# The operands of an MLP made five steps ahead instead of four, the fifth pair in fixed buffers

## The chip, the cores and the metric

The kernel runs on one core of one Trainium2 chip. TensorE (PE) multiplies matrices; VectorE (DVE) and ScalarE (ACT) work element by element; GpSimd (POOL) here mostly issues transfers that add into a tile; SyncE (SP) issues the other transfers. The metric is the device time of one execution in microseconds (us), lower is better.

## What is computed

A two-layer encoder over 512 positions of width 1024: stick-breaking attention in layer 0, a gated linear recurrence (RG-LRU) in layer 1, and behind each a MLP with squared ReLU and 4096 inner features. The change touches the MLPs alone, and their seams to what comes next:

```python
def squared_relu_mlp(h, w1, w2):
    u = jax.nn.relu(h @ w1)
    return (u * u) @ w2

def reference(x, ...):
    for layer in range(2):
        h = rms_norm(x, norm_mix[layer])
        y = stick_breaking_attention(h, ...) if layer == 0 else rglru_block(h, w_in, ...)
        x = x + y
        h = rms_norm(x, norm_mlp[layer])
        x = x + squared_relu_mlp(h, mlp_w1[layer], mlp_w2[layer])
    return rms_norm(x, norm_final)
```

## The kernel before

**Three matmuls for one.** PE multiplies a rounded 32-bit type. Each operand is held as a high half (the value rounded by a cast on ACT, `wh` for a weight, `sh` or `bh` for an activation) and a low half (what the rounding left, a subtraction on DVE: `wl`, `sl`, `bl`). A product is high times high, low times high, high times low.

**Seven products for eight.** The MLP's 4096 features are worked through in four quarters of 1024. In each quarter the up product and the down product are done on 2 by 2 blocks with seven products P1 to P7 in place of eight, for two halves p (or g) of the weights. A step is one product of one half: "P1 1" is P1 of half 1. A quarter has 14 up steps (places 0 to 13: P1 P5 P6 P3 P7 P2 P4 for p = 0, then for p = 1) and 14 down steps (places 14 to 27, in the order of `ORDERS`); the first quarter's up part is done in another way, so its steps begin at place 14. A step number i counts from the first quarter's first down step; `STEPS // 2`, 14, is the second quarter's first up step.

**Weight blocks.** `load` asks SP for blocks of 512 KB (`b11`, `b12`, `b22`, each with a buffer of its own) at fixed places. P2's block `b21` goes to a tile `raw` of the pool `wpool` instead, which has three such tiles. `added` makes the sums of blocks that some products need: the block itself is overwritten, by DVE (`b<-b,b`) or, for P7 and P4, by a transfer that POOL issues and that adds what it reads from memory. `operand` then makes a pair `wh`, `wl`; there are four pairs in turn. The stages behind the MLP take their weights through `slab`, with the same pairs and the same three raw tiles: `w_in` behind layer 0.

**Order.** In `run`, slot i is: `load(i)`, then `leave(i - 1)`, then PE's matmuls of step i. `leave` takes a finished step's result out of PSUM (ACT copies, DVE sums, `collect` into the output `c`), then calls `prepare(ahead)`, which makes the operand of a later step, here four steps on, with the block sums due, and then does what is left: relu, square, and the halves of the squared activations (`split`, `split_slot`, whose `sl` the down steps read). On ACT and DVE the instructions of the MLP run strictly in the order in which they are written (class `Ordered`); each engine starts nothing before the instruction ahead of it. SP and POOL have orders of their own, and a transfer into a buffer waits until its former content has been read.

**The end of layer 0.** The last steps' `leave` finds no more operands to make. The next stage begins with two slabs of `w_in`, whose `wl` (line 251) stand in DVE's order among the last `collect`s; behind them come the sums into `x` (line 1426) and the halves `xg` (lines 166 and 167) that the new stage's matmuls (lines 257 to 259) read.

Of the kernel before, what the change touches and what calls it, by code (L numbers as in the profile page):

```python
# [13 lines left out]
F32R = mybir.dt.float32r  # L14
# [53 lines left out]
def hybrid_encoder(  # L68
# [739 lines left out]
    class Mlp:  # L808
# [28 lines left out]
        def __init__(self, ctx, layer):  # L837
            self.layer, self.sq, self.first = layer, Squares(), None
            self.V, self.A = Ordered(V), Ordered(A)
            self.mp = ctx.enter_context(tc.tile_pool(name=f"mlp{layer}", bufs=2))  # L840
            self.c = [
                self.mp.tile([P, 2, S], F32, tag=f"c{i}", name=f"c{i}", bufs=1) for i in range(4)
            ]
            self.begun, self.a, self.aside = set(), {}, {}
            self.turns = count(4 * layer)
            self.blocks = ExitStack()
            self.bp = self.blocks.enter_context(tc.tile_pool(name=f"blocks{layer}", bufs=2))
            self.u, self.lows, self.s3, self.slots = {}, {}, {}, None

            t = self.bp.tile([P, C // 2 * S + ASIDE], F32R, tag="s41", name="s41", bufs=1)  # L850
            self.s41 = t[:, : C // 2 * S].rearrange("p (k s) -> p k s", s=S)
# [237 lines left out]
            )  # L1089

        def operand(self, raw):
            pool = wpools[next(slabs) % len(wpools)]
            wh = pool.tile([P, C, P], F32R, tag="wh", name="wh")
            wl = pool.tile([P, C, P], F32R, tag="wl", name="wl")
            wh, wl = (t.rearrange("p (j k) f -> p j (k f)", j=2) for t in (wh, wl))
            self.A.copy(wh, raw)
            self.V.tensor_tensor(wl, raw, f(wh), ALU.subtract)
            return wh, wl
# [73 lines left out]
        def run(self, first, between, end):  # L1172
# [47 lines left out]
            def prepare(i):  # L1220

                if i < len(steps) and steps[i][0] == "up" and steps[i][3] == "P7":
                    return
                if i - 1 in range(len(steps)) and i - 1 not in made and i > 2:
                    make(i - 1)
                if i < len(steps) and steps[i][0] == "down":
                    add(i, 0)
                    if waiting and place(i) in (20, 22, 23):
                        self.split_slot(*waiting.pop(0))
                make(i)  # L1230
                for n in range(i + 1, i + 6):
                    add(n, n - i)
# [4 lines left out]

            def load(i):
                q4, at = steps[i][1], place(i)
                for do in self.aside.get(i, ()):  # L1240
                    do()

# [2 lines left out]
                elif at == 0:  # L1245
                    self.turns = count(4)
                    self.u.clear()
                    del self.a[1]
                elif at == 4:
                    units["down", q4] = self.from_down(q4)  # L1250
                    self.load(units["down", q4], (0, "b11"), (0, "b12"), (1, "b11"))
                elif at == 11:
                    self.load(units["down", q4], (1, "b12"), (0, "b22"), (1, "b22"))
                elif at == 14 and q4 == NQ - 1:
                    end.ready()
                elif at == 22 and q4 < NQ - 1:
                    units["up", q4 + 1] = self.from_up(q4 + 1)
                    self.load(units["up", q4 + 1], (0, "b11"), (0, "b12"), (0, "b22"), (1, "b11"))
                elif at == 25 and q4 < NQ - 1:
                    self.load(units["up", q4 + 1], (1, "b12"), (1, "b22"))  # L1260

            def leave(i):

                ahead = i + 4
                if i < 0:
                    return
                kind, q4, p, name = steps[i]
# [627 lines left out]
```

## Time and profile before

| what | us |
| --- | --- |
| median of 3 runs (lowest, highest) | 1002.76 (1002.46, 1003.22) |
| the profiled execution | 1003.18 |
| its span, first to last instruction | 1001.3 |
| PE busy in it | 983.0 |
| DVE busy | 858.0 |
| ACT busy | 715.4 |

The granted clock of TensorE was 0.999 of full speed over the span. The page groups the helper classes' instructions under line 798, so the tiles' names tell them apart. The groups and transfers of the MLPs' weights:

```profile
L798 ACT CAST wh<-b 128x1024 fp32r<-128x1024 f32 x168 | 173.7, 1048 | 99.6 <-DVE b L798 50.1
L798 DVE TENSOR_TENSOR wl<-b,wh 128x1024 fp32r<-128x1024 f32 x168 | 203.6, 1220 | 38.9 <-ACT wh L798 38.5
L798 DVE TENSOR_TENSOR b<-b,b 128x1024 f32<-128x1024 f32 x48 | 58.7, 1223 | 1.3
L798 ACT CAST wh<-raw 128x1024 fp32r<-128x1024 f32 x46 | 47.9, 1043 | 4.1 <-PE ps_acc L1135 4.0
b<-in_w_dn SPq DMA_DIRECT2D x48, 512.0 KB, 5.1
b<-in_w_up POOLq DMA_DIRECT2D x24, 512.0 KB, 5.8
```

A row of a group has the engine, the operation, output and inputs with their shapes, how many; then busy us and the mean of one in ns; then how long the engine stood idle just before them and on whose account. A row of transfers ends with its size and the median us from issue to landing. A row of a timeline has the start in us, the length of the run of equal instructions, the instruction, how many, and in brackets the idle time before it and what ended it. A row of waits has the instruction that waited, what released it, the sum, how many times and the longest.

### The profile page before, as it was taken

Reading aid. Unit: us, or ns where it says so; the run is one execution under the profiler, and the core shown is the slowest. Engines: PE = TensorE matmul, PEld = TensorE weight load, DVE = VectorE, ACT = ScalarE, POOL = GpSimd, SP = SyncE. Lnnn points to the kernel's source line nnn. Section 1 sums busy time; section 2 is a strip of 40 time slices with the busy share of each in tenths; the row PEclk is TensorE's granted clock in tenths of the full one; section 3 lists DMA queues with packets and bytes.
Section 4 is the critical chain, followed back from the end, with each engine's and each line's share of the span. In section 5 each row is a group of like instructions: output and inputs, shape, how many; then the busy total and the mean of one; then the engine's idle time right before and its main releaser. Section 6 shows DMA issues by size and latency. Waiting matters only on the chain.

```text
span 1001.3 us, 15918 instructions
## 1 busy us (share of the span) xinstructions
PE 983.0 (98%) x5836; PEld 884.0 (88%) x5836; DVE 858.0 (86%) x1152; ACT 715.4 (71%) x1110; POOL 176.4 (18%) x243
## 2 busy tenths in 40 slices
PE   9999999999999999999999999999999999999996
PEld 7889999888878988988988888888889989989985
DVE  6888787848898799799799799986887898998898
ACT  6777676836887774774775699975887774874865
POOL 0454444420000011011011220100011111111111
PEclk9999999999999999999999999999999999999999
DMA  7855454537637767777693474446548877977953
GB/s 230 216 146 148 106 153 109 160 117 256 174 87 198 169 160 198 169 163 194 169 239 88 128 191 126 124 157 223 122 95 219 212 142 202 249 141 199 229 107 106
DMA packets 71902, 165.72 MB, mean 166 GB/s; under 512 B 23824, under 2 KB 25104, under 8 KB 71824
## 3 DMA queue, kind: packets, MB, share of 16 engines
q1 hardware_dynamic: 59424, 123.54, 39.4%
q0 software_dynamic: 11680, 40.38, 24.0%
q8 instruction: 46, 0.75, 0.3%
q10 hardware_dynamic: 720, 0.79, 0.2%
q14 instruction: 32, 0.26, 0.1%
HBM read 139.51 MB, written 6.29 MB: 146 GB/s over the span
## 4 chain that ended last, share of the span: by engine, by line
PE 39%; DVE 25%; ACT 22%; issue 8%; DMA 6%; SPq 0%; ACTq 0%; POOL 0%; DVEq 0%; POOLq 0%
PE ps_t L1135 8%; DVE wl L798 6%; ACT wh L798 6%; PE ps_acc L1135 4%; DVE u L798 4%; ACT u L798 3%; PE ps_acc L1036 3%; DVE b L798 3%; PE ps_acc L257 3%; PE ps_acc L259 3%; PE ps_acc L258 2%; PE ps_z L1135 2%; ACT bh L798 2%; DVE c L798 2%; ACT L798 2%
## 5 line engine op out<-in xcount | busy, mean ns | idle before, releaser
L798 ACT CAST wh<-b 128x1024 fp32r<-128x1024 f32 x168 | 173.7, 1048 | 99.6 <-DVE b L798 50.1
L798 DVE TENSOR_TENSOR wl<-b,wh 128x1024 fp32r<-128x1024 f32 x168 | 203.6, 1220 | 38.9 <-ACT wh L798 38.5
L1113 POOL DMA_DIRECT2D b<-in_w_dn x40 | 35.0, 876 | 339.6 <-DVE b L798 153.1
L1036 PE MATMUL ps_z<-xg,wh 128*128 128x256 f32 x384 | 78.2, 277 | 1.0 <-ACT u L798 1.0
L257 PE MATMUL ps_acc<-xg,wh 128*128 128x512 f32 x200 | 79.1, 395 | 0.0
L259 PE MATMUL ps_acc<-xg,wh 128*128 128x512 f32 x200 | 75.8, 379 | 0.0
L258 PE MATMUL ps_acc<-xg,wl 128*128 128x512 f32 x200 | 75.8, 379 | 0.0
L251 DVE TENSOR_TENSOR wl<-raw,wh 128x512 fp32r<-128x512 f32 (+2 forms) x70 | 62.0, 911 | 15.1 <-ACT wh L249 14.8
L798 ACT ACTIVATE u<-u 128x512 f32<-128x512 f32 x100 | 63.2, 632 | 13.3 <-DVE u L798 11.6
L623 DVE TENSOR_TENSOR_SCAN scan<-keep,later 128x128 f32<-128x128 f32 (+1 forms) x64 | 59.3, 929 | 12.9 <-ACT keep L613 6.5
L1036 PE MATMUL ps_z<-xg,wl 128*128 128x256 f32 x240 | 66.0, 275 | 0.0
L1036 PEld LDWEIGHTS ps_z<-xg,wh 128*128 128x128 f32 x384 | 63.5, 192 | 1.7 <-ACT u L798 1.6
L249 ACT CAST wh<-raw 128x512 fp32r<-128x512 f32 (+2 forms) x70 | 50.5, 757 | 19.1 <-PE ps_acc L259 6.8
L627 POOL TENSOR_TENSOR w<-w,scan 128x128 f32<-128x128 f32 (+1 forms) x64 | 51.6, 807 | 53.6 <-DVE scan L623 50.6
L1036 PE MATMUL ps_acc<-xg,wh 128*128 128x256 f32 x288 | 60.5, 275 | 0.0
L798 DVE TENSOR_TENSOR b<-b,b 128x1024 f32<-128x1024 f32 x48 | 58.7, 1223 | 1.3
L798 DVE TENSOR_TENSOR u<-u 128x512 f32<-128x512 f32 (+1 forms) x92 | 54.8, 595 | 2.3 <-ACT u L798 1.0
L1113 POOL DMA_DIRECT2D b<-in_w_up x24 | 20.9, 869 | 196.8 <-DMA b<-in_w_up 84.4
L1036 PE MATMUL ps_acc<-xg,wl 128*128 128x256 f32 x192 | 52.8, 275 | 0.0
L1036 PE MATMUL ps_acc<-low,wh 128*128 128x256 f32 x192 | 52.8, 275 | 0.0
L798 ACT CAST wh<-raw 128x1024 fp32r<-128x1024 f32 x46 | 47.9, 1043 | 4.1 <-PE ps_acc L1135 4.0
L1135 PE MATMUL ps_t<-wh,sl 128*128 128x512 f32 x126 | 48.5, 385 | 1.9 <-DVE sl L798 1.9
(372 smaller groups left out, 3257.9 us busy)
## 6 DMA issues: line engine op xcount, KB each, us to landing
b<-in_w_dn SPq DMA_DIRECT2D x48, 512.0 KB, 5.1
b<-in_w_dn POOLq DMA_DIRECT2D x40, 512.0 KB, 5.5
b<-in_w_up SPq DMA_DIRECT2D x36, 512.0 KB, 4.7
b<-in_w_up POOLq DMA_DIRECT2D x24, 512.0 KB, 5.8
raw<-in_w_m SPq DMA_DIRECT2D x16, 512.0 KB, 4.7
raw<-in_w_dn SPq DMA_DIRECT2D x16, 512.0 KB, 4.9
raw<-in_w_in SPq DMA_DIRECT2D x16, 512.0 KB, 4.2
raw<-in_w_qk SPq DMA_DIRECT2D x12, 512.0 KB, 3.7
```

Source lines behind the costliest of these rows:

```text
L249: A.copy(wh[:, k, :], raw[:, k, :])
L251: V.tensor_tensor(wl[:, k, :], raw[:, k, :], f(wh[:, k, :]), ALU.subtract)
L257: PE.matmul(ps, wh, ah, start=start, stop=False)
L258: PE.matmul(ps, wl, ah, start=False, stop=False)
L259: PE.matmul(ps, wh, al, start=False, stop=stop)
L623: V.tensor_tensor_scan(sc[:, S - n : S][:, ::-1], keep[:, :n][:, ::-1], later[:, S - n :][:, ::-1], 1.0, ALU.mult, ALU.max,)
L627: G.tensor_tensor(wt, wt, sc[:, S - n + 1 : S + 1], ALU.mult)
L798: ins = getattr(self.e, name)(*args, **kwargs)
L1036: PE.matmul(as_read(ps[:, i * HS : (i + 1) * HS]), m, turns_of(y), start=new and i == k == n == 0, stop=i == 1 and k == C // 2 - 1 and n == 2,
L1113: G.dma_start(out=unit[b].rearrange("p j n -> p (j n)"), in_=unit["src"](to), accum_op=ALU.add)
L1135: PE.matmul(ps, m, y[:, jj], start=first and n == 0, stop=last and n == 2, skip_group_check=not new,)
```

## The change

From the second quarter's first up step on, `leave` prepares five steps ahead. Every fifth operand from then on (the 15th, counted from nought, and so on) takes a fixed pair `spare` in place of the turn's; it lies in two of the three raw tiles and stays there to the end of the MLP. The places at which `split_slot` is called in `prepare` and the blocks are asked for are moved on or back by one, so that `split_slot` stays in the same slot and the blocks are asked for one slot sooner. `operand` takes the pairs from `wpool` directly, where it counted with `slab` before; the list of pools had one member.

```diff
-            self.turns = count(4 * layer)
+            self.turns, self.operands, self.spare = count(4 * layer), count(), None
...
         def operand(self, raw):
-            pool = wpools[next(slabs) % len(wpools)]
-            wh = pool.tile([P, C, P], F32R, tag="wh", name="wh")
-            wl = pool.tile([P, C, P], F32R, tag="wl", name="wl")
+            n = next(self.operands)
+            if n >= self.STEPS // 2 and n % 5 == 0:
+                if self.spare is None:
+                    self.spare = [
+                        wpool.tile([P, C, P], F32R, tag="raw", name="spare", bufs=3) for _ in range(2)
+                    ]
+                wh, wl = self.spare
+            else:
+                wh = wpool.tile([P, C, P], F32R, tag="wh", name="wh")
+                wl = wpool.tile([P, C, P], F32R, tag="wl", name="wl")
...
-                    if waiting and place(i) in (20, 22, 23):
+                    if waiting and place(i) in (21, 23, 24):
                         self.split_slot(*waiting.pop(0))
...
+                sooner = i >= self.STEPS // 2
...
-                elif at == 4:
+                elif at == 4 - sooner:
...
-                elif at == 11:
+                elif at == 11 - sooner:
...
-                elif at == 22 and q4 < NQ - 1:
+                elif at == 22 - sooner and q4 < NQ - 1:
...
-                elif at == 25 and q4 < NQ - 1:
+                elif at == 25 - sooner and q4 < NQ - 1:
...
-                ahead = i + 4
+                ahead = i + (5 if i >= self.STEPS // 2 else 4)
```

What this does to the engines' orders, at three places. First DVE at the end of the up part in layer 0's last quarter, before the change; `ps_o` is PE's sum for P3 in the first row and for P2 in the eighth, the last row's `sl` is the one made from P2's result:

```order
L798 TENSOR_TENSOR u_5617<-ps_o_5652,u_5617 128x512
L798 TENSOR_TENSOR wl_5753<-b11_5505,wh_5752 128x1024
L798 TENSOR_TENSOR b11_5505<-b11_5505,b12_5507 128x1024
L798 TENSOR_TENSOR u_5618<-u_5618,u_5619 128x512
L798 TENSOR_TENSOR sl_5786<-u_5617,sh_5785 128x2x256
L798 TENSOR_TENSOR wl_5790<-b11_5505,wh_5789 128x1024
L798 TENSOR_TENSOR sl_5786<-u_5618,sh_5785 128x2x256
L798 TENSOR_TENSOR u_5616<-u_5616,ps_o_5799 128x512
L798 TENSOR_TENSOR wl_5826<-b11_5509,wh_5825 128x1024
L798 TENSOR_TENSOR b11_5509<-b11_5509,b12_5745 128x1024
L798 TENSOR_TENSOR sl_5786<-u_5616,sh_5785 128x2x256
```

The same engine and place with the change:

```order
L798 TENSOR_TENSOR b11_5456<-b11_5456,b12_5458 128x1024
L798 TENSOR_TENSOR bl_79<-u_5367,bh_78 128x1024
L798 TENSOR_TENSOR u_5591<-ps_o_5636,u_5591 128x512
L798 TENSOR_TENSOR spare_3839<-b11_5456,spare_3838 128x1024
L798 TENSOR_TENSOR u_5592<-u_5592,u_5593 128x512
L798 TENSOR_TENSOR sl_5764<-u_5591,sh_5763 128x2x256
L798 TENSOR_TENSOR wl_5768<-b11_5460,wh_5767 128x1024
L798 TENSOR_TENSOR b11_5460<-b11_5460,b12_5692 128x1024
L798 TENSOR_TENSOR sl_5764<-u_5592,sh_5763 128x2x256
L798 TENSOR_TENSOR u_5590<-u_5590,ps_o_5776 128x512
L798 TENSOR_TENSOR wl_5805<-raw_5802,wh_5804 128x1024
L798 TENSOR_TENSOR sl_5764<-u_5590,sh_5763 128x2x256
```

Each weight half and each add has moved one slot forward: the first add stands ahead of P3's sum, the second ahead of P2's sum, where it stood behind it.

Second ACT in the second quarter of layer 0, the first in which five ahead holds. The copies of `ps_acc` are those of P1, P5 and P6, and the last that of P7; `b11_3745` is the block into which a transfer of POOL's adds. Before:

```order
L798 COPY u_3879<-ps_acc_3880 128x2x256
L798 COPY u_3879<-ps_acc_3906 128x2x256
L798 CAST wh_3932<-b12_3747 128x1024
L798 CAST wh_3938<-raw_3936 128x1024
L798 COPY u_3879<-ps_acc_3880 128x2x256
L798 CAST wh_3967<-b11_3745 128x1024
L798 CAST wh_4002<-b11_3751 128x1024
L798 ACTIVATE u_3879<-u_3879 128x2x256 x2
L798 COPY u_3879<-ps_acc_3880 128x2x256
```

The same with the change:

```order
L798 COPY u_3879<-ps_acc_3880 128x2x256
L798 CAST wh_3906<-b12_3747 128x1024
L798 CAST wh_3912<-raw_3910 128x1024
L798 COPY u_3879<-ps_acc_3916 128x2x256
L798 CAST spare_3838<-b11_3745 128x1024
L798 COPY u_3879<-ps_acc_3880 128x2x256
L798 CAST wh_3975<-b11_3751 128x1024
L798 CAST wh_4005<-b11_3751 128x1024
L798 ACTIVATE u_3879<-u_3879 128x2x256 x2
L798 COPY u_3879<-ps_acc_3880 128x2x256
```

The cast of `b11_3745` has moved ahead of P6's copy, and a cast of an added block (the second of `b11_3751`) ahead of P7's.

Third SP at the end of layer 0, before the change; `x` are rows of the residual that come back from memory, `raw<-in_w_in` the next stage's slabs:

```order
L243 DMA raw_6173<-in_w_in 128x1024
L1449 DMA x_5866<-away_3141 128x512
L1449 DMA x_5868<-away_3141 128x512
L1066 DMA b22_5749<-in_w_dn 128x1024
L1449 DMA x_5870<-away_3141 128x512
L243 DMA raw_6179<-in_w_in 128x1024
L243 DMA raw_6265<-in_w_in 128x1024
```

With the change:

```order
L1457 DMA x_5848<-away_3141 128x512
L1112 DMA raw_5992<-in_w_dn 128x1024
L243 DMA raw_6141<-in_w_in 128x1024
L243 DMA raw_6147<-in_w_in 128x1024
L243 DMA raw_6233<-in_w_in 128x1024
```

The first slab stood ahead of three other loads and now stands behind them and behind the last block `b21` of the MLP (`raw_5992`), with which it shares the one raw tile that is left. Where these slabs' `wl` stand on DVE with the change:

```order
L798 TENSOR_TENSOR spare_3839<-raw_5992,spare_3838 128x1024
L798 TENSOR_TENSOR wl_6009<-b11_5456,wh_6008 128x1024
L798 SCALAR_TENSOR_TENSOR c1_3132<-ps_acc_5883,rr_3492,c1_3132 128x512
L798 SCALAR_TENSOR_TENSOR c1_3132<-ps_acc_5884,rr_3492,c1_3132 128x512
L798 TENSOR_TENSOR wl_6027<-b11_5460,wh_6026 128x1024
L798 SCALAR_TENSOR_TENSOR c3_3134<-ps_t_5864,rr_3492,c3_3134 128x512
L251 TENSOR_TENSOR wl_6144<-raw_6141,wh_6143 128x1024
L798 SCALAR_TENSOR_TENSOR c3_3134<-ps_t_5865,rr_3492,c3_3134 128x512
L798 SCALAR_TENSOR_TENSOR c0_3131<-ps_z_5922,rr_3492,c0_3131 128x512
L798 SCALAR_TENSOR_TENSOR c0_3131<-ps_z_5923,rr_3492,c0_3131 128x512
L251 TENSOR_TENSOR wl_6150<-raw_6147,wh_6149 128x1024
L798 SCALAR_TENSOR_TENSOR c2_3133<-ps_t_5864,rr_3492,c2_3133 128x512
```

The next rows are the sums into `x` (line 1426 before, 1434 with the change), as they were; of the slabs' two `wl`, the first has moved ahead of one `collect`, the second stands where it stood.

## Prediction

> **What bounds the kernel now.** I read the page first (busy shares), then PE's waits, then the timelines of PE, DVE and ACT around them.
>
> ```profile
> PE 983.0 (98%) x5836; PEld 884.0 (88%) x5836; DVE 858.0 (86%) x1152; ACT 715.4 (71%) x1110; POOL 176.4 (18%) x243
> PE ps_t L1135 <- DVE sl L798: 1.9, 6, 0.3
> PE ps_z L1036 <- ACT u L798: 0.8, 2, 0.6
> ```
>
> TensorE (PE) is busy for 98% of the span; the change leaves its matmuls as they are, so only its waits can move. Those in the MLPs are short (the last row is of the window from 555 to 900 us alone). PE stands for `sl` (the low half of the squared activations) once in each of six quarters. The last quarter of layer 0 shows how:
>
> ```profile
> 513.99 0.38 PE L1135 MATMUL ps_t<-wl,sh 128*128 128x512 f32 x1
> 514.69 0.48 PE L1135 MATMUL ps_t<-wh,sl 128*128 128x512 f32 x1 [0.32 <-DVE sl L798]
> 515.01 0.38 PE L1135 MATMUL ps_t<-wh,sh 128*128 128x512 f32 x1
> 516.95 0.38 PE L1135 MATMUL ps_z<-wh,bh 128*128 128x512 f32 x1
> 517.42 0.48 PE L1135 MATMUL ps_z<-wl,bh 128*128 128x512 f32 x1
> 517.74 0.38 PE L1135 MATMUL ps_z<-wh,bl 128*128 128x512 f32 x1
> ```
>
> Undisturbed, these matmuls start every 0.216 us (nine of them from 515.01 to 516.95). In step "P1 1" (product P1, half 1) the one due at 514.21 came at 514.69, 0.48 late, and the next lost 0.10 more. In "P2 0" the second lost 0.25, the third 0.10. That is 0.94 us a quarter, of which only 0.35 is for a weight half `wl`, what the change makes earlier; 0.58 is for `sl`.
>
> **Where the late `sl` comes from.** DVE, then ACT, in the same quarter:
>
> ```profile
> 493.03 1.76 DVE L798 TENSOR_TENSOR bl<-u,bh 128x1536 fp32r<-128x1536 f32 x1 [1.48 <-ACT bh L798]
> 494.70 1.22 DVE L798 TENSOR_TENSOR wl<-b,wh 128x1024 fp32r<-128x1024 f32 x1
> 495.84 2.86 DVE L798 TENSOR_TENSOR u<-u 128x512 f32<-128x512 f32 x4
> ...
> 504.29 0.69 DVE L798 TENSOR_TENSOR u<-ps_o,u 128x512 f32<-128x512 f32 x1
> 504.89 1.22 DVE L798 TENSOR_TENSOR wl<-b,wh 128x1024 fp32r<-128x1024 f32 x1
> 506.14 1.22 DVE L798 TENSOR_TENSOR b<-b,b 128x1024 f32<-128x1024 f32 x1
> ...
> 510.35 0.69 DVE L798 TENSOR_TENSOR sl<-u,sh 128x512 fp32r<-128x512 f32 x1 [0.61 <-ACT sh L798]
> 510.96 0.68 DVE L798 TENSOR_TENSOR u<-u,ps_o 128x512 f32<-128x512 f32 x1
> ...
> 512.81 1.23 DVE L798 TENSOR_TENSOR b<-b,b 128x1024 f32<-128x1024 f32 x1
> 513.95 0.68 DVE L798 TENSOR_TENSOR sl<-u,sh 128x512 fp32r<-128x512 f32 x1
> ```
>
> ```profile
> 511.67 1.30 ACT L798 ACTIVATE u<-u 128x512 f32<-128x512 f32 x2 [0.41 <-DVE u L798]
> 513.00 0.62 ACT L798 CAST sh<-u 128x512 fp32r<-128x512 f32 x1
> ```
>
> From 493.03 to 514.63 DVE stands for 0.61 us only: here DVE's queue is the limit. The `u` of 510.96 (P2's sum) releases ACT's relu and square, these `sh`, and that the `sl` at 513.95, whose end at 514.63 PE waits for.
>
> **Part 1, five steps ahead, in a settled quarter: +0.8 us.** No instruction is added. What moves one step forward is each cast, its `wl` and the add behind it (`b<-b,b`). In DVE's order the `wl` of 494.70 goes before the `bl`, so the four sums follow at 494.65. Behind them now stand `wl` three times, `bl`, `wl`, the add of a step further, `bl` (today `wl` twice, `bl`, `wl`, `bl`). Behind such an operation the next starts 1.14 us later (512.81 to 513.95), the add 1.25 behind the `wl` that still reads its block (504.89 to 506.14). So `u<-ps_o,u` comes at 505.5 instead of 504.29. Its relu, square and `sh` (1.30 + 0.62) end at 508.2, `sl` follows; the next `wl` waits for its cast (1.05) until 509.2, then stands an add (1.25), a `sl`, and P2's `u` at 512.2, against 510.96. Relu, square and `sh` then end at 514.85 and `sl` at 515.55. It is only 0.9 late against 514.63 because today's `sl` waits behind the add of 512.81, which is now past. PE loses those 0.9 at "P1 1" and wins the 0.35 at "P2 0": +0.55. A second place adds 0.25: in the slot behind "P5 0" the add, its cast and the `wl` into the fixed pair now follow each other, with 1.1 us of DVE idle, and the `sl` that "P6 1" needs at about 526.05 ends near 526.3. So +0.8 a quarter; the ends are +0.4 (no second wait) and +1.2 (P4's step waits as well, for a copy that now stands behind a cast of the added block, as in part 2).
>
> **Part 2, the first quarter with five ahead, once in each layer: +2.4 and +1.9 us.** P7's step takes its PSUM bank when ACT has copied P6's result out of it.
>
> ```profile
> 329.08 0.59 ACT L798 COPY u<-ps_acc 128x512 f32<-128x512 f32 x1 [0.20 <-PE ps_acc L1036]
> 330.77 2.03 ACT L798 CAST wh<-b 128x1024 fp32r<-128x1024 f32 x2 [1.11 <-DMA b<-in_w_up]
> 331.56 0.28 PE L1036 MATMUL ps_acc<-xg,wh 128*128 128x256 f32 x1
> 336.92 0.28 PE L1036 MATMUL ps_acc<-xg,wh 128*128 128x256 f32 x1
> 776.61 2.02 ACT L798 CAST wh<-b 128x1024 fp32r<-128x1024 f32 x2 [1.22 <-DMA b<-in_w_up]
> 777.28 0.28 PE L1036 MATMUL ps_acc<-xg,wh 128*128 128x256 f32 x1
> ```
>
> The first of the two casts reads a block into which a POOL transfer accumulates. Its landing, at 330.77, follows the operand before it, which the first quarter doesn't make sooner. The change puts that cast ahead of the copy of 329.08. ACT takes its work in order, so the copy runs from 331.75 to 332.35 and P7's step starts 0.8 late against 331.56. ACT and DVE start the next casts and adds later by as much, and the copy that P4's step (336.92) needs now stands behind a cast that waits for an add: it ends near 338.7, where 337.7 is due, another 1.0. The settled quarter's 0.6 follows at its end: 2.4. In layer 1 the two are 0.87 (778.15 against 777.28) and 1.1; 0.6 follows and about 0.7 of the 0.8 that PE waits there for ACT's `u` today (the window's row above) is absorbed: 1.9. Later quarters make the operand a step sooner, the transfer lands before the cast's turn, and the term goes.
>
> **Part 3, the end of layer 0: +3.7 us.** The fixed pair leaves one of the three raw tiles for loads. Three of w_in's blocks come through these tiles for the next stage.
>
> ```profile
> 517.39 18.11 SPq L243 DMA_DIRECT2D raw<-in_w_in x2
> 533.93 1.22 DVE L798 TENSOR_TENSOR wl<-raw,wh 128x1024 fp32r<-128x1024 f32 x1
> 540.82 1.05 ACT L249 CAST wh<-raw 128x1024 fp32r<-128x1024 f32 x1 [1.54 <-PE ps_z L1135]
> 542.42 1.22 DVE L251 TENSOR_TENSOR wl<-raw,wh 128x1024 fp32r<-128x1024 f32 x1
> 544.22 1.28 DVE L1426 TENSOR_TENSOR x<-x,ps_z 128x512 f32<-128x512 f32 x2
> 546.61 1.41 DVE L167 SCALAR_TENSOR_TENSOR xg<-x,colt,xg 128x512 fp32r<-128x512 f32 x2
> 547.98 0.38 PE L259 MATMUL ps_acc<-xg,wh 128*128 128x512 f32 x1
> raw<-in_w_in SPq DMA_DIRECT2D x3, 512.0 KB, 3.5
> raw<-in_w_m SPq DMA_DIRECT2D x16, 512.0 KB, 4.7
> ```
>
> The stage begins with two of them; the second, cast at 540.82, is asked for at 517.39 today. Changed, the first is asked for when the `wl` of 533.93 is done (near 536.3, with the quarter's lateness), and the second when the first's `wl` is done. By the row before the last (535 to 546 us) a load takes 3.5: 536.3 + 3.5 + 1.05 + 1.22 = 542.1, and again 5.8 later: 547.9. In DVE's order this second `wl` still stands ahead of the adds into x of 544.22, which so start at 548.55, 4.3 late. The low halves `xg` end today at 547.36 (first of two, from 546.61), 0.6 before PE needs them at 547.98. So PE comes 3.7 late, this quarter's own +0.8 within it. Ends: 0.8 if the loads are somehow in time; 6.1 with 4.7 us a load, the last row (the page's median for other weights).
>
> [...]
>
> **Part 4, the last quarter of layer 1: -0.2 us.** It waits for `wl` twice:
>
> ```profile
> 974.55 0.38 PE L1135 MATMUL ps_t<-wh,sh 128*128 128x512 f32 x1
> 974.99 0.48 PE L1135 MATMUL ps_t<-wl,sh 128*128 128x512 f32 x1
> ...
> 977.46 0.38 PE L1135 MATMUL ps_acc<-wh,bh 128*128 128x512 f32 x1
> 978.04 0.48 PE L1135 MATMUL ps_acc<-wl,bh 128*128 128x512 f32 x1 [0.20 <-DVE wl L798]
> ```
>
> By the starts 0.22 and 0.36 beyond 0.216, and 0.10 behind each: 0.78. This goes, and about 0.6 for `sl`, as in a settled quarter, comes.
>
> **At nothing:** block loads asked for a step sooner. They land in about 5 us and are used two steps or more later, beside PE's work; with that cover gone, they could delay an accumulating transfer by about 1 us in each first quarter. The renumbered places of `split_slot` keep its turn.
>
> **Sum.** One settled quarter in each layer (0.8 each), first quarters 2.4 + 1.9, end of layer 0 3.7, last quarter -0.2: 9.4 us. The profiled execution took 1003.18 (span 1001.3 and 1.9 around it), so 1012.6; the median of the runs, 1002.76, lies 0.4 under it: **1012.2**.
>
> **The rivals.** (a) Faster: PE loses both waits, because `sl` comes in time. It decides at 514.2: if `sl` of P2 ends by then in a settled quarter, 0.94 goes in five quarters, 0.78 in the last and the 0.8 for ACT's copies in layer 1: 6.3, so 996.5; with part 3's wait kept (3.7 less its own 0.8), 999.4. For it: weight halves a step earlier take work off DVE in the slots behind. Against it: the same queue must do one more add before that `sl`. (b) The first quarters and settled ones as forecast, the seam hidden (0.8): 1009.3. For it: SP may ask earlier if DVE is less late. (c) The change brings nothing: the fixed pair comes free no sooner than the pairs it relieves, gains and losses cancel: 1002 to 1004. (d) All terms at their upper ends: 9.4, 2.4 for part 3, 0.4 in four settled quarters and 1 in each first one: 15.4, 1018.
>
> **How the numbers follow.** Forecast 0.58, (a) 0.14, (b) 0.12, (c) 0.10, (d) 0.06. Leaving out (a) and (d) leaves 0.80, so the range goes from 1002 to 1017. A measurement here tells about 0.2%, 2 us: faster 0.14, same 0.10, slower 0.76.
>
> **What will show it.** Right: PE's wait for `sl` at "P1 1" about 1.4 instead of 0.48 and none at "P2 0"; in each first quarter an ACT cast released by DMA ahead of the copy, PE late at P7 and P4; at 548 the L1434 adds of x behind a `wl` whose load was issued near 542. Wrong: `sl` done as early as today, or w_in's loads issued before 535.

## The result and the profile after

| kernel | median us (lowest to highest) | ratio to before, 95% interval |
| --- | --- | --- |
| before, beside the changed kernel | 1002.78 (1002.46 to 1003.22) | |
| changed | 1026.57 (1023.63 to 1028.36) | 1.0236 [1.0222, 1.0250] |
| changed, a second set beside a before of 1002.01 | 1024.89 (1024.20 to 1026.13) | 1.0228 [1.0214, 1.0242] |

The change costs 23.8 us where 9.4 were forecast: the direction was right, the size far outside the range. The profiled execution of the changed kernel took 1026.18, its span is 1024.3, 23.0 more than before. The page's busy row, and its costliest new group:

```profile
PE 989.3 (97%) x5836; PEld 888.0 (87%) x5836; DVE 860.6 (84%) x1152; ACT 711.9 (70%) x1110; POOL 176.1 (17%) x243
L1142 PE MATMUL ps_t<-wh,bh 128*128 128x512 f32 x106 | 42.7, 403 | 10.8 <-DVE c L798 10.8
```

PE issues the same 5836 matmuls, yet is busy 6.3 us longer (983.0 before). The same number of matmuls with more busy time points to slower ones here; the clock further down shows it. And one kind of matmul, the first of a down step with `wh` and `bh`, now waits 10.8 us in all for a `c`, a sum that DVE makes out of PSUM; before, no wait for `c` stood among PE's larger ones. The view of PE's waits with the change (sum, times, longest):

```profile
PE ps_t L1142 <- DVE c L798: 10.8, 6, 2.0
PE ps_z L1036 <- ACT u L798: 4.0, 6, 1.0
PE ps_t L1142 <- ACT sh L798: 3.7, 6, 0.6
PE ps_acc L1036 <- ACT u L798: 2.9, 4, 0.8
```

The other three rows are the waits that the prediction's parts 1 and 2 spoke of. The first row it did not have.

**Where the 23.0 us arise.** PE's steps come in the same order in both kernels, so the start of each step's first matmul can be compared one by one. The shift grows by:

| stretch | forecast | measured |
| --- | --- | --- |
| ahead of the changed slots | 0 | -2.0 |
| layer 0, second quarter (first with five ahead) | 2.4 | 6.66 |
| layer 0, third quarter | 0.8 | 3.06 |
| layer 0, last quarter, and on to layer 1's MLP | 3.7 | 4.73 + 0.97 |
| layer 1, second quarter | 1.9 | 5.99 |
| layer 1, third quarter | 0.8 | 3.30 |
| layer 1, last quarter to the end | -0.2 | 0.31 |

The -2.0 is not the change's: these slots are the same in both kernels, and in the other profiles of them the shift lies between -1.9 and +0.3.

In five of the six quarters step "P6 0" (product P6, half 0) alone adds 2.20, and in three of these five the step itself takes 1.76 longer: 11.0 and 5.3 of the 23.0.

**What happens at "P6 0".** The timeline of DVE, then that of PE, in the changed kernel's layer 0, last quarter:

```profile
527.61 1.22 DVE L798 TENSOR_TENSOR wl<-b,wh 128x1024 fp32r<-128x1024 f32 x1
528.74 1.22 DVE L798 TENSOR_TENSOR b<-b,b 128x1024 f32<-128x1024 f32 x1
531.12 1.23 DVE L798 TENSOR_TENSOR spare<-b,spare 128x1024 fp32r<-128x1024 f32 x1 [1.17 <-ACT spare L798]
532.26 1.40 DVE L798 SCALAR_TENSOR_TENSOR c<-ps_t,rr,c 128x512 f32<-128x512 f32 x2
```

```profile
530.74 0.38 PE L1142 MATMUL ps_acc<-wh,sl 128*128 128x512 f32 x1
533.16 0.45 PE L1142 MATMUL ps_t<-wh,bh 128*128 128x512 f32 x1 [2.03 <-DVE c L798]
...
533.67 0.63 PE L1142 MATMUL ps_t<-wh,bl 128*128 128x512 f32 x1
534.10 0.63 PE L1142 MATMUL ps_t<-wh,bh 128*128 128x512 f32 x1
```

And the same place before the change, DVE and PE:

```profile
520.76 0.75 DVE L798 SCALAR_TENSOR_TENSOR c<-ps_t,rr,c 128x512 f32<-128x512 f32 x1
521.42 1.22 DVE L798 TENSOR_TENSOR b<-b,b 128x1024 f32<-128x1024 f32 x1
...
522.27 0.38 PE L1135 MATMUL ps_acc<-wh,sl 128*128 128x512 f32 x1
```

"P6 0" adds onto a `ps_t` bank that holds a result of P1, which the first `c` has to read first. Before, that `c` ended at 521.51 (520.76 + 0.75), while "P6 0" was due at 522.49, one matmul (0.22) behind the last row, which is the end of "P5 1": 0.98 to spare. With the change DVE has its `wl` behind it 2.00 ahead of that last matmul (528.74 against 530.74), before 1.51 ahead (520.76 against 522.27), so 0.49 sooner. But then it does an add for "P6 1", stands 1.17 until ACT has cast the added block, and makes the `wl` into the fixed pair: 3.52 us from 528.74 to 532.26, all ahead of the `c`. So the `c` is 3.03 later (3.52 less 0.49), 2.05 more than there was to spare, and PE's restart has 0.15 of its own: 2.20.

That the pair is the fixed one is so in this quarter alone. In the other four the operand of "P6 1" is an ordinary pair, with the same standing ahead of its `wl` (layer 0, second quarter):

```profile
373.85 1.23 DVE L798 TENSOR_TENSOR wl<-b,wh 128x1024 fp32r<-128x1024 f32 x1 [1.17 <-ACT wh L798]
```

So the order costs this, not the buffer.

The matmuls behind the wait then start 0.43 us apart instead of 0.216. The view of windows has the granted clock in the column behind POOL's (us, then busy time and count of PE, weight loads, DVE, ACT, POOL, then the clock, the DMA share, GB/s); each row begins with "P6 0" and goes on for 4.4 or 4.5 us, in layer 0's quarters two, three and four and layer 1's two and three:

```profile
376.00:380.40 4.40, 4.40 (x13) 3.57 (x14) 4.40 (x6) 1.87 (x4) 0.34 (x1) 0.61 0.98 172
455.30:459.80 4.50, 4.43 (x21) 3.92 (x22) 4.50 (x6) 1.97 (x4) 0.56 (x1) 1.00 0.95 163
533.10:537.60 4.50, 4.44 (x13) 3.65 (x14) 4.50 (x6) 1.97 (x4) 0.53 (x1) 0.62 0.96 154
837.00:841.50 4.50, 4.42 (x13) 3.62 (x14) 4.50 (x6) 1.97 (x4) 0.56 (x1) 0.62 0.96 159
917.00:921.50 4.50, 4.50 (x21) 3.96 (x22) 4.50 (x6) 1.97 (x4) 0.47 (x1) 1.00 0.99 174
```

Where the mean clock of the row is 0.61 to 0.62, 13 matmuls fit where otherwise 21 do. A narrower window shows what the mean is made of: half the clock, for 3.41 us, which is about 1.7 us lost.

```profile
376.63:380.04 3.41, 3.41 (x10) 2.69 (x9) 3.41 (x5) 1.28 (x2) 0.00 (x0) 0.50 1.00 161
```

It is so in three of the five places, beginning 0.2 to 0.8 us after PE resumed, though the wait ahead was 2.03 or 2.04 in all five.

### The profile page after: what moved, and what is told of

Same layout as the page of the kernel before. It is cut to its first block, busy times and chain, and to the rows that moved or that the text cites. A ratio compares the mean times of both kernels' runs of the same rounds, so it can differ in the third digit from the quotient of the medians.

```text
span 1024.3 us, 15910 instructions
## 1 busy us (share of the span) xinstructions
PE 989.3 (97%) x5836; PEld 888.0 (87%) x5836; DVE 860.6 (84%) x1152; ACT 711.9 (70%) x1110; POOL 176.1 (17%) x243
## 4 chain that ended last, share of the span: by engine, by line
PE 44%; DVE 23%; ACT 18%; DMA 7%; issue 7%; SPq 1%; ACTq 0%; DVEq 0%; POOL 0%; POOLq 0%
PE ps_t L1142 10%; PE ps_acc L1036 6%; DVE wl L798 5%; ACT wh L798 4%; PE ps_acc L1142 3%; ACT u L798 3%; DVE b L798 3%; PE ps_z L1036 3%; DVE u L798 3%; PE ps_acc L257 2%; PE ps_acc L259 2%; PE ps_acc L258 2%; DVE bl L798 2%; ACT L798 2%; DVE c L798 2%
## 5 line engine op out<-in xcount | busy, mean ns | idle before, releaser
L798 ACT CAST wh<-b 128x1024 fp32r<-128x1024 f32 x137 | 142.5, 1047 | 88.5 <-DVE b L798 65.2
L798 DVE TENSOR_TENSOR wl<-b,wh 128x1024 fp32r<-128x1024 f32 x137 | 166.4, 1219 | 40.0 <-ACT wh L798 39.8
L1036 PE MATMUL ps_z<-xg,wh 128*128 128x256 f32 x304 | 62.2, 276 | 3.0 <-ACT u L798 3.0
L798 ACT CAST spare<-b 128x1024 fp32r<-128x1024 f32 x31 | 32.4, 1046 | 34.7 <-DVE b L798 21.3
L1036 PEld LDWEIGHTS ps_z<-xg,wh 128*128 128x128 f32 x304 | 50.5, 192 | 3.7 <-ACT u L798 3.7
L1142 PE MATMUL ps_t<-wh,bh 128*128 128x512 f32 x106 | 42.7, 403 | 10.8 <-DVE c L798 10.8
L1036 PE MATMUL ps_z<-xg,wl 128*128 128x256 f32 x192 | 52.8, 275 | 0.0
L1036 PE MATMUL ps_acc<-xg,wh 128*128 128x256 f32 x224 | 49.3, 276 | 1.4 <-ACT u L798 1.4
L798 ACT CAST wh<-raw 128x1024 fp32r<-128x1024 f32 x43 | 44.8, 1044 | 4.8 <-issue 2.8
L798 DVE TENSOR_TENSOR spare<-b,spare 128x1024 fp32r<-128x1024 f32 x31 | 37.8, 1218 | 10.6 <-ACT spare L798 10.6
```

The lines of the kernel that those rows point to most:

```text
L798: ins = getattr(self.e, name)(*args, **kwargs)
L1036: PE.matmul(as_read(ps[:, i * HS : (i + 1) * HS]), m, turns_of(y), start=new and i == k == n == 0, stop=i == 1 and k == C // 2 - 1 and n == 2,
L1142: PE.matmul(ps, m, y[:, jj], start=first and n == 0, stop=last and n == 2, skip_group_check=not new,)
```

## The experiments

**The add and the `wl` for "P6 1" behind the two sums `c`.** In five quarters the operand of "P6 1" is made a slot later, so that the two `c` of P1 come first; all else as in the changed kernel.

```diff
...
+                    mid = i >= self.STEPS // 2 and not (self.layer and q4 == NQ - 1)
+                    late = i + 4 if mid and place(i) == 16 else ahead
-                    if steps[min(ahead, len(steps) - 1)][0] == "down":
-                        add(ahead, 0)
+                    if steps[min(late, len(steps) - 1)][0] == "down" and not (mid and place(i) == 15):
+                        add(late, 0)
...
-                    prepare(ahead)
+                    if late != ahead:
+                        self.split_slot(*waiting.pop(0))
+                        prepare(late)
+                    if not (mid and place(i) == 15):
+                        prepare(ahead)
```

> One operand, that of P6 1, is made a slot later again, so that on DVE the two sums c<-ps_t of P1 1 stand ahead of its wl; all else stays five ahead. Theory A (the wait of 2.2 us at P6 0 comes from the order of those sums behind add, cast and wl, and the half clock of the next 4 us from that wait): PE waits for c no more, no stretch has a granted clock near 0.6, 5 x 2.2 and 3 x 1.8 go from the profiled 1026.2; the x adds at the end of layer 0 are then uncovered and cost about 3: 1013, and 1010 if they stay covered. Theory B (DVE is late as a whole by 2 us, whichever is first): PE's wait turns up at P6 0 or P6 1 for wl or sl with most of its length, 1020 or more.

Measured: 1017.28 (1016.51 to 1020.18), ratio 1.0156 [1.0139, 1.0172]. The profile is of the fastest run, 1016.51: all five waits at "P6 0" and the half clock behind them are gone from it. Some 8 to 9 us came back, less than expected (the time lies between the two theories), because other waits came (view of PE's waits):

```profile
PE ps_acc L1142 <- DVE c L798: 2.0, 5, 0.4
PE ps_acc L259 <- DVE xg L167: 1.0, 1, 1.0
PE ps_acc L257 <- ACT xg L166: 0.7, 1, 0.7
```

DVE now reaches the sums for "P3 0" late (0.55 by the starts, five times), and the end of layer 0 shows 2.0 us of waiting, by the same comparison, that the changed kernel hides (part 3 below).

**Only the standing time taken out of that place.** The add for "P6 1" goes ahead of the `wl` of "P6 0", so its cast is ready when DVE comes to the `wl` of "P6 1". What DVE has to do ahead of the `c` stays.

```diff
+                    if i >= self.STEPS and place(i) == 14 and not (self.layer and q4 == NQ - 1):
+                        add(i + 6, 0)
```

> The changed kernel, with the add for P6 1 one place earlier on DVE, ahead of P6 0's wl, so that its cast runs beside that wl and DVE no longer stands 1.17 us between add and wl. Theory A (PE's wait at P6 0 is what DVE does and stands ahead of the sums of c, us for us): the wait falls from 2.2 to about 1.0 in five quarters, no half clock follows a wait that short, and the end of layer 0 comes uncovered by about 2: 1026.6 - 5.8 - 5.3 + 2 = 1017.5. Theory B (the wait is set by PE's or ACT's side, such as the cast into the fixed pair waiting for the pair's last reader): it stays near 2 us, 1024 or more.

Measured: 1019.25 (1018.19 to 1020.58), ratio 1.0166 [1.0151, 1.0182]. The timeline of DVE in the same quarter, and PE's first row of "P6 0":

```profile
526.70 1.22 DVE L798 TENSOR_TENSOR wl<-b,wh 128x1024 fp32r<-128x1024 f32 x1
527.95 1.23 DVE L798 TENSOR_TENSOR spare<-b,spare 128x1024 fp32r<-128x1024 f32 x1
529.09 1.40 DVE L798 SCALAR_TENSOR_TENSOR c<-ps_t,rr,c 128x512 f32<-128x512 f32 x2
...
529.98 0.46 PE L1142 MATMUL ps_t<-wh,bh 128*128 128x512 f32 x1 [0.90 <-DVE c L798]
```

No bracket stands at the `spare` row any more, and "P6 0" adds 1.06 instead of 2.20 in each of the five quarters: the difference, 1.14, is the 1.17 of standing. None of the five places has the half clock. But the end of layer 0 now shows 2.76 of waiting, and the half clock stands behind that, behind two waits of 1.43 and 1.00 that begin 1.7 us apart (window view):

```profile
559.27:562.68 3.41, 3.41 (x14) 2.97 (x13) 3.06 (x5) 3.41 (x6) 2.67 (x3) 0.50 0.00 0
```

That costs another 1.7, and explains most of what lies between the 1017.5 expected and the 1019.25 measured.

**Matmuls that nobody reads, in place of the wait.** Nine matmuls of 128x512 into a free bank ahead of "P6 0" in the five quarters; they wait for nothing and take 9 x 0.216 = 1.94 us, the wait's own time.

```diff
+                    if i >= self.STEPS and place(i) == 19 and not (self.layer and q4 == NQ - 1):
+                        for n in range(2):
+                            ps = bank("o")
+                            for m in range(5 - n):
+                                PE.matmul(ps, ...)
```

> The changed kernel with 9 matmuls more in each of the five quarters with a wait of 2.2 us at P6 0, put just ahead of it into a PSUM bank that nobody reads, 1.9 us that PE would stand. Theory A (the half clock follows from PE standing about 2 us): no stretch with a granted clock near 0.6 in any quarter, PE's wait for c 0.3 to 0.4 instead of 2.0, time 1026.6 less 1.8 for each of the about three quarters with half a clock: 1021, runs closer to each other than 1023.6 to 1028.4. Theory B (the clock is lowered for another reason, such as the transfers there): half clock stays, 1024 to 1028.

Measured: 1022.50 (1021.83 to 1022.59), ratio 1.0205 [1.0189, 1.0220]. PE in layer 0's last quarter, and the window behind it:

```profile
529.30 2.26 PE L1382 MATMUL ps_o<-wh,bh 128*128 128x512 f32 x9
531.41 0.48 PE L1142 MATMUL ps_t<-wh,bh 128*128 128x512 f32 x1
```

```profile
531.40:535.80 4.40, 4.40 (x21) 3.88 (x21) 4.40 (x6) 1.87 (x3) 0.57 (x1) 1.00 0.92 154
```

"P6 0" is still 2.11 late by the starts, but the clock is 1.00 in all five places of this one profile, and the four runs lie within 0.8 us, where the changed kernel's two sets spread over 4.7 and 1.9. With 7 falls in 16 such waits elsewhere, five places without one would come by chance about once in 18 times; that in e1 and e10 the clock stays up at these places too, once the wait is gone or short, speaks for the wait as the cause. The time is 20.5 over the kernel before where the changed kernel is 22.9 and 23.8 over its own: 2.3 to 3.3 less. That is under the 5.3 of three half clocks, partly because the end of layer 0 shows more of its wait here (1.17 instead of 0.41; part 3 below).

**The changed kernel once more**, unedited, for the clock.

> The changed kernel once more, unedited. A (whether the clock halves behind each wait of P6 0 is chance of the moment; each time it does costs 1.7 to 1.8 us): the five waits of 2.0 at P6 0 are there again, but the quarters with a granted clock near 0.6 behind them need not be the three of the first profile; single times lie between about 1021 (none) and 1030 (all five), in all runs with five waits, and spread over more than 3 us. B (the clock's fall belongs to the three quarters): the same three again, and times within 1 us of each other.

Measured: 1024.89 (1024.20 to 1026.13), as in the table above. The spread of 1.9 us lies between the two expectations. The profile decides: the five waits of 2.03 to 2.04 are there, but only two places have the half clock. Layer 0's second quarter, with half the clock in the first profile, has all of it in this one; layer 0's last and layer 1's second quarter fall in both (window view, steps "P6 0" of layer 0's quarters two and four):

```profile
376.40:380.80 4.40, 4.40 (x21) 3.86 (x22) 4.40 (x6) 1.87 (x4) 0.45 (x1) 1.00 0.94 161
532.00:536.40 4.40, 4.40 (x13) 3.57 (x14) 4.40 (x6) 1.87 (x4) 0.44 (x1) 0.61 0.91 156
```

By the starts the second quarter grows by 4.80 here instead of 6.66. The profiled execution is 1.55 us shorter (1024.63 against 1026.18), of the size of one fall, 1.76, though the runs of the kernel before differ by as much too (1001.14 to 1003.34 in this set).

**The fixed pair alone, four steps ahead.**

```diff
-                    if waiting and place(i) in (21, 23, 24):
+                    if waiting and place(i) in (20, 22, 23):
...
-                sooner = i >= self.STEPS // 2
+                sooner = 0
...
-                ahead = i + (5 if i >= self.STEPS // 2 else 4)
+                ahead = i + 4
```

> Four steps ahead as before and blocks asked for as before; only the fixed pair in two raw tiles is kept. Theory A (part 3 of the prediction, covered in the changed kernel by PE's own lateness): waits in the quarters as before the change, and at the end of layer 0 w_in's first slab asked for near 535, its second near 541, PE's first matmul with the low xg 2.6 us late: 1005.4. Theory B (the raw tiles cost nothing, all is the order): 1002 to 1003.

Measured: 1005.46 (1004.61 to 1006.83), ratio 1.0034 [1.0022, 1.0045]. The quarters are as before within 0.5 us. The end of layer 0 waits, as part 3 of the prediction had it, for the halves `xg` behind the slabs (view of PE's waits):

```profile
PE ps_acc L259 <- DVE xg L167: 1.7, 1, 1.7
```

And layer 1's last quarter loses 2.7 at three steps that wait for a `wl`: with one raw tile left, SP asks for a block `b21` only at 963.23 there, and ACT stands 4.11 for it. That the time meets the expected 1005.4 is luck: the end of layer 0 costs 1.90 by the starts where 2.6 was expected, and nobody expected the 2.7. So the fixed pair has a price of its own, but a small one; most of the loss comes with the fifth step.

**Blocks asked for a step sooner, alone**, in the kernel before.

```diff
+                sooner = i >= self.STEPS // 2
-                elif at == 4:
+                elif at == 4 - sooner:
...
```

> The kernel before with the blocks asked for a step sooner, nothing else. Theory A: nothing waits for these blocks, 1002 to 1003 like before. Theory B: they stand in the way of the transfers that add, +1 in each layer: 1004.5.

Measured: 1002.01 against 1001.96, ratio 0.9999 [0.9990, 1.0008]. Nothing.

**Five ahead begun later**: from the third quarter's first step on, and from place 23 of the second quarter.

```diff
-                ahead = i + (5 if i >= self.STEPS // 2 else 4)
+                ahead = i + (5 if i >= 42 else 4)
```

The fixed pair, `sooner` and `split_slot`'s places follow the same bound; the second kernel has 37 for 42.

> Five ahead only from the third quarter's first up step on. Theory A (the late P7 and P4 steps come from the switch at a quarter's first up step: the transfer that adds has no head start yet): second quarters as before the change, third quarters late by 0.8 at P7 and at P4 of half 0, where the changed kernel has no wait there; second quarter's 6.7 and 6.0 go, 1.7 come in each third: 1026.2 - 12.7 + 3.4 = 1017. Theory B (these waits belong to the second quarter, whose data come late for another reason): no wait at P7 and P4 of the third quarter, and the second quarter keeps some of its lateness: 1013.5 or above 1019.

> Five ahead from place 23 of the second quarter's down part on (where DVE and ACT stand idle), so that the third quarter's first operands have their head start. Theory A: no PE wait at P7 and P4 of half 0 anywhere, third quarters late by about 3.1 to 3.3 as in the changed kernel: 1026.2 - 12.7 = 1013.5. Theory B (a switch costs its 1.7 wherever it is): 1017, like a switch at the quarter's start.

Measured: 1020.32 (1017.79 to 1022.22), ratio 1.0187 [1.0170, 1.0204], and 1019.11 (1017.41 to 1020.28), ratio 1.0167 [1.0152, 1.0183]. The second quarter of each layer is as before in the first, and loses only the entry in the second; every later quarter but layer 1's last has its 2.20 at "P6 0", and each profile has one half clock. Neither time is one that the expectations gave (1020.32 against 1017 by A, 1013.5 or over 1019 by B; 1019.11 against 1013.5 and 1017). The entry is not what part 2 made of it: begun in the third quarter, P7 comes in time and only P4 is late, 0.50 and 1.11; begun at place 23, neither is late, but "P4 0" of the down part loses 1.32 in each layer, and the end of layer 0 shows its wait again in the second kernel (3.2 where the changed kernel has 0.97). So the entry costs 0.5 to 2 us in each of the three places tried.

**Five ahead except in the slots behind the late `sl`** (four ahead from place 9 to 16).

```diff
+                back = i >= self.STEPS // 2 and 9 <= place(i) <= 16
+                ahead -= back
```

> Five ahead as in the change, but four ahead from place 9 to 16 of each quarter (P6 1's operand at place 16 again behind the sums of c). Theory A (part 1: the operand and add of a step further lie ahead of P3's and P2's sums on DVE and of ACT's copy, only there, where DVE is the limit): the waits for ACT's u at P4 of half 1 (0.4 to 1.1) and for sh at P1 1 (0.8) and the 0.55 for c at P3 0 that e1 has go, those of before (0.94 a quarter) come back; what stays are P7 and P4 in the second quarters (1.4 and 1.9) and the end of layer 0 (about 2): 1007. Theory B (five ahead itself is late, wherever it is): 1013 or more.

Measured: 1014.34 (1013.72 to 1014.95), ratio 1.0123 [1.0109, 1.0137]. The added waits at "P4 1" and "P1 1" are gone and so are those at "P6 0", but P3's step now waits for its `c` (view of PE's waits):

```profile
PE ps_acc L1142 <- DVE c L798: 4.3, 5, 0.9
```

By the starts 1.03 in each of five quarters. The settled quarters nevertheless cost little: 0.43 and 0.11 in layer 0's third and last quarters and 0.94 in layer 1's third, where the changed kernel has 3.06, 4.73 and 3.30. The rest of the loss is the entry (2.3 and 1.8), the end of layer 0 (2.5) and layer 1's last quarter: that loses 3.66 from P6 to P7, 1.83 of it in one wait for a `c` at "P7 0", and wins 0.8 back at "P4 0". The time lies at the lower edge of theory B (1013 or more), but what it lost is not spread over every place, as B had it; most of it is entry and seam, as A had it (1007), plus a last quarter that A did not have.

**Can the same queue be made shorter at all?** In the kernel before, four ahead: P2's sum goes ahead of P7's `sl` on DVE, P2's `sl` ahead of the add, and P4's operand is made first in its slot. No work is taken out.

```diff
+                while name == "P2" and p and lows:
+                    lows.pop(0)()
+                if name == "P4" and p:
+                    prepare(ahead)
...
-                prepare(ahead)
+                if not (name == "P4" and p):
+                    prepare(ahead, adds=not (name == "P2" and p))
...
+                    if name == "P2" and p:
+                        for n in range(ahead + 1, ahead + 6):
+                            add(n, n - ahead)
```

> The kernel before, four ahead, with another order at the end of each up part: on DVE P2's sum ahead of P7's sl, P2's sl ahead of the add, and P2 0's operand ahead of P4's relu on ACT. Theory A (DVE's order around P2's sum sets the late sl): sl of P2 ends near 513.8 where 514.2 is due and wl of P2 0 near 515.3, both waits go, 0.94 in up to six quarters: 997.5 to 999 against 1002.1 to 1002.8. Theory B (DVE has as much to do anyway, the wait turns up at the next step, P5 1 or P6 0): less than 1 us faster.

Measured: 1003.53 (1002.42 to 1005.23), ratio 1.0019 [1.0010, 1.0028]. Theory A (997.5 to 999) fails. The two waits of 0.48 and 0.25 at P1 and P2 are gone, and "P5 1" has one of up to 0.8 for its `wl` (view of PE's waits):

```profile
PE ps_acc L1142 <- DVE wl L798: 5.7, 9, 0.8
```

DVE stands 0.26 and 0.62 in that stretch, where it stood 0.61 and 0.18 before: the order changed who waits, not how much DVE has to do. The same with the add back ahead of P2's `sl`:

```diff
-                    prepare(ahead, adds=not (name == "P2" and p))
+                    prepare(ahead)
```

> e5 with the add back ahead of P2's sl: DVE stands only about 0.3 instead of 0.9 us between bl and P5 1's wl. Theory A (PE's wait is DVE's backlog, and only standing time taken out of it is won): P1 1 waits about 0.3 for sl, P2 0 and P5 1 next to nothing, 0.5 a quarter less than before: 999.5 to 1000.5 against 1002. Theory B (ACT's chain is as long, DVE's standing time turns up elsewhere): like before or like e5, 1002 to 1003.5.

> The kernel of e6_reorder2 once more, since 0.2% is near what a comparison tells. A (DVE's standing time was taken out): about 2 us under the kernel before again, 999.5 to 1000.7 where before is near 1002.3, and DVE standing 0.3 us or less in the stretch in which it stood 0.61. B (the 0.2% was chance): within 0.8 us of before.

Measured: 1000.17 (998.02 to 1001.43), ratio 0.9979 [0.9970, 0.9988], and again 1000.25 (998.90 to 1002.46), ratio 0.9982 [0.9973, 0.9991]. (One of the first eleven runs took 4720.76 and is in no ratio; none of the second eleven did.) This is 0.2% faster than the kernel before, and so faster than the changed one too. The timeline of DVE in the second run of it, in the same quarter:

```profile
507.09 0.68 DVE L798 TENSOR_TENSOR u<-u,ps_o 128x512 f32<-128x512 f32 x1
507.79 0.69 DVE L798 TENSOR_TENSOR sl<-u,sh 128x512 fp32r<-128x512 f32 x1
508.74 1.22 DVE L798 TENSOR_TENSOR wl<-b,wh 128x1024 fp32r<-128x1024 f32 x1 [0.26 <-ACT wh L798]
509.99 1.22 DVE L798 TENSOR_TENSOR b<-b,b 128x1024 f32<-128x1024 f32 x1
511.14 0.68 DVE L798 TENSOR_TENSOR sl<-u,sh 128x512 fp32r<-128x512 f32 x1
```

DVE stands 0.26 from 507.09 to the end of P2's `sl` at 511.83, because P2's sum is done early enough for ACT's relu and square to run while DVE does an add. In the version before this one it stood 0.62 more there.

## Why the prediction was right or wrong

**What bounds the kernel: right.** DVE's queue is the limit in that stretch, and more work ahead of a sum costs PE time (a `c` 3.03 later, "P6 0" 2.20). The reordered kernels say the same from the other side: with DVE's standing at 0.26 the time is 1000.25 against 1002.01.

**Part 1, the settled quarter: the first place right in sum, the second wrong.** Up to "P5 1" the third and last quarters lose 0.79 and 0.77 in layer 0, 1.03 and 1.07 in layer 1, where the part's +0.55, or +0.4 to +1.2 with its ends, was expected. That the sums agree is partly luck. P4's step ("P4 1") waits for ACT's copy, which only the upper end had: 0.54 to 0.60 in layer 0 and about 1.0 in layer 1. PE comes later to "P1 1" by that, so "P1 1" and "P2 0" together add only 0.13 to 0.23. And at "P1 1" PE waits first for ACT's `sh` (0.63) and then about 0.3 for `sl`, where 1.4 for `sl` was forecast; the wait at "P2 0" is gone as forecast.

The step that failed is the sentence "A second place adds 0.25: in the slot behind "P5 0" the add, its cast and the `wl` into the fixed pair now follow each other, with 1.1 us of DVE idle, and the `sl` that "P6 1" needs". The 1.1 us were there (1.17), and the sequence too, though the fixed pair is in it in one quarter only. But the prediction followed only the `sl` behind it to its reader. Between the two stand the sums `c`, and the reader of what they free is a step earlier, "P6 0". Its bank was 0.98 us ahead of need before; 3.03 later, it costs 2.20 a quarter, in five quarters 11.0. Putting the add and the `wl` behind the sums takes the wait away; taking only the standing out takes 1.14 of it away.

**A term that no part had: the clock.** Behind a wait of 2.0 us PE's granted clock fell to 0.50 for 3.41 us in 7 of the 16 such waits of four profiles, 1.76 us by the starts; behind the waits of 0.9 at "P6 0" in none of five, but once behind the two close waits of 1.43 and 1.00. With unread matmuls in the wait's place it did not fall in five places. Why it fell behind some of the waits and not behind others is not shown. So such a place costs 2.20, or 3.96 where the clock falls, as long as that covers no later wait (part 3).

**Part 2, the first quarters: the chain right, but not for the reason that they are first.** The cast that waits for the transfer stands ahead of the copy that frees P7's bank (ACT's timeline, then PE's, of the changed kernel, layer 0):

```profile
328.77 1.05 ACT L798 CAST spare<-b 128x1024 fp32r<-128x1024 f32 x1 [3.80 <-DMA b<-in_w_up]
329.73 0.58 ACT L798 COPY u<-ps_acc 128x512 f32<-128x512 f32 x1
...
330.36 0.38 PE L1036 MATMUL ps_acc<-xg,wh 128*128 128x256 f32 x1 [0.65 <-ACT u L798]
```

P7 is 0.82 late and P4 0.83 (forecast 0.8 and 1.0); in layer 1, 0.90 and 1.00 (0.87 and 1.1). Of old waits for ACT's `u` 1.15 go in layer 1 (0.7 expected). The transfer took 6.4 us, and the 0.82 goes with the 3.80 for which ACT stands for it; in five other profiles of the same quarter ACT stands 3.34, 3.52, 3.63, 3.79 and 3.79, and P7 is 0.36, 0.54, 0.64, 0.80 and 0.80 late, so the size was partly luck. From the landing to P7's start the cast and the copy take 1.66, so P7 is late when the transfer lands less than that ahead of P7's time: here it landed 0.84 ahead. With the switch in the third quarter P7 isn't late: there the transfer, asked for 7.5 us ahead, took only 5.44 and 5.75 and landed 2.10 and 1.79 ahead. So what decides here is the time of the landing, not that the quarter is the first with five ahead; why the transfer was shorter there is not shown.

**Part 3, the end of layer 0: the chain right, but for the most part hidden.** SP, ACT, DVE and PE there, with the change:

```profile
544.41 8.94 SPq L243 DMA_DIRECT2D raw<-in_w_in  x3
554.75 1.05 ACT L249 CAST wh<-raw 128x1024 fp32r<-128x1024 f32 x1 [5.57 <-DMA raw<-in_w_in]
555.83 1.22 DVE L251 TENSOR_TENSOR wl<-raw,wh 128x1024 fp32r<-128x1024 f32 x1 [1.83 <-ACT wh L249]
557.64 1.27 DVE L1434 TENSOR_TENSOR x<-x,ps_z 128x512 f32<-128x512 f32 x2
560.82 0.48 PE L259 MATMUL ps_acc<-xg,wh 128*128 128x512 f32 x1 [0.25 <-DVE xg L167]
```

From the first load's issue to the sums into `x` it is 13.2 us (544.41 to 557.64), forecast 12.25 (536.3 to 548.55); the two loads took 3.6 and 3.4, forecast 3.5. But the first is asked for earlier than forecast against PE's steps: 544.41 less the 12.4 by which PE is late there is 532.0 in the times of before, and the forecast's 536.3 less its 0.8 is 535.5. Only 0.41 of the wait is left, so the forecast's 2.9 (3.7 less the quarter's own 0.8) is not seen. Most of this is the half clock in that quarter, which makes PE's step 1.76 longer and leaves SP's request where it was: 11.25 us behind the start of "P6 0" with it (544.41 less 533.16), 11.35 without it (542.76 less 531.41, with the unread matmuls):

| kernel | growth in layer 0's last quarter | half clock there | wait left at its end, by the starts |
| --- | --- | --- | --- |
| changed, changed once more, begun in the third quarter | 4.7 | yes | 0.41, 0.52, 0.36 |
| begun at place 23 | 3.05 | no | 2.56 |
| unread matmuls | 2.99 | no | 1.17 |
| add for "P6 1" first | 1.92 | no | 2.76 |
| add and `wl` for "P6 1" behind the sums | 1.37 | no | 2.0 |

So a half clock in that quarter adds little to the whole, because it covers a wait that otherwise shows: quarter and seam (the end of layer 0 and on to layer 1's MLP) together cost 5.70 with it, and without it 6.25 begun at place 23 and 4.73 with the unread matmuls. Rival (b), the seam hidden, came about, though for a reason that it did not name. Counted against PE's steps, so did the sign that was to show the forecast wrong, a load of `w_in` issued before 535.

**Part 4: its two terms came, and two more.** The 0.78 of the old waits for `wl` goes; 1.07 for the settled chain comes, and 0.84 at P7 for a `c`. About 0.8 of an older wait at "P4 0" goes, which the prediction did not have; without it the 0.31 would be near 1.1. "P6 0" has no wait there.

**At nothing: right.** The loads asked for sooner change nothing (1002.01 against 1001.96); the 1 us by which they might delay a transfer in each first quarter was the author's estimate, and it does not show.

**The rivals.** Rival (a) needed a `sl` in time and would be 996.5; DVE's rows show it later. Rival (d), all upper ends, still lies over 8 us under the measurement: the range was made of the ends of waits that had been found, and had no room for one that hadn't.

## What to carry to other kernels

An operand made a step sooner is not free when the engine that makes it works in order, as DVE and ACT do here: each instruction that moved forward delayed what it passed, and what it passed freed a PSUM bank (the `c` comes 3.03 later, "P6 0" 2.20) or fed another engine (P2's sum feeds ACT, for whose `sh` PE waits 0.63 at "P1 1"). So when work moves forward, list every instruction that it passes, find the reader of each, and compare the delay with the time that each had to spare; here one subtraction, 3.03 against 0.98, was left out, for the one reader that mattered. And time was won in this queue by taking out the time in which DVE stood, as the reordered kernel did (1000.17 and 1000.25 against 1002.25 and 1002.01), not by choosing who waits (1003.53 against 1001.96).

## What the runs showed of the hardware

Behind PE standing 2.03 to 2.04 us the granted clock fell to 0.50 for 3.41 us in 7 of 16 cases (four profiles); in the changed kernel's profile this began 0.2 to 0.8 us after PE resumed. Two waits of 1.43 and 1.00, 1.7 us apart, were followed by the same once; two of 1.22 and 1.00 (begun at place 23), and single waits of 0.90 at "P6 0" and of 1.74 at the end of layer 0 (the fixed pair alone), were not. Between executions of one program the places differ (three of five in one profile of 1026.18, two of five in another of 1024.63). With nine matmuls that nobody reads in place of the wait the clock was 1.00 in five of five places. The kernel with the add behind the sums, without such waits in its profile, still spread over 3.7 us in four runs; the mean granted clock of its two longer runs was 0.996 and 0.997 against 0.999 in the shorter two, so a fall may be in them, but they were not profiled.
